# Low parts of MLP weights: negated high part plus an adding transfer, in place of a subtraction on GpSimd

## Chip, cores and metric

The kernel runs on one core of a Trainium2 chip. The metric is the device time of one execution in microseconds (us). The time before is the median of three runs, 1112.05 us.

## What is computed

One layer of a hybrid encoder on 512 tokens of width 1024, in float32: a token mixer (a Mamba-2 branch, windowed attention, gates, an output product) and then a squared-ReLU MLP with a hidden width of 4096. The change touches only the MLP:

```
h = rmsnorm(x, pre_mlp_norm[l])
f = jnp.square(jax.nn.relu(h @ w_mlp_in[l])) @ w_mlp_out[l]
x = x + rmsnorm(f, post_mlp_norm[l])
```

w_mlp_in is 1024 x 4096 and w_mlp_out is 4096 x 1024.

## The kernel before

**Split products.** TensorE multiplies in fp32r, which keeps fewer bits than float32. So every factor is split into a high part (the value rounded to fp32r) and a low part (the value less its high part), and each product is three matmuls, `mm3` in lines 350 to 354: high by high, high by low, low by high, added up in PSUM. A weight chunk of 128 partitions by 1024 columns (512 KB) is loaded from HBM into a raw tile `wr` (`chunk_raw`, line 399, on SP's queue). ScalarE rounds it into `wh` (line 419), and GpSimd subtracts, `wl = wr - wh`, in pieces of 256 columns (line 423). `wr`, `wh` and `wl` have three buffers each (RAW and SPL of line 27); chunk n takes the buffer of chunk n - 3 once the last matmul that reads it is done.

**The MLP.** The hidden width is cut into 32 blocks of 128, one "up quantum" each (`up_quantum`, lines 1335 and 1336, which calls `cm`): one chunk of w_mlp_in in 8 slices of 128 x 128, 24 matmuls into one PSUM bank. The first three up quanta are made in two halves of the tokens (`up_halves`). Then `up_done` squares the result. Blocks 0 to 23 form three parts of eight. The second product of such a part is "folded": a two by two block scheme with seven products in place of eight (`folded_quanta`). A folded product has two chunks of its own, made of w_mlp_out rows by sums and differences (tiles `wd` and `wt`), with ScalarE's rounding in line 1413 and GpSimd's subtraction in line 1416, four pieces of 256 columns a chunk; it too has 24 matmuls. The last part (blocks 24 to 31) is the plain quarter: eight chunks of w_mlp_out through the same `chunk_split` (`down_quanta`, line 1453).

**The order of the work.** In `build` (lines 1561 to 1566) each of the seven folded products of a part is followed by one up quantum of the next part, and an eighth up quantum stands at the part's end. So the rings of three `wh` and three `wl` buffers go round once per pair: two chunks for the folded product, one for the up quantum. An up quantum's chunk takes the buffers of the up quantum before it, and one folded product runs on TensorE between the two.

**The planner.** All instructions are recorded first. `Planner` (lines 76 to 275) then simulates them with a cost per instruction (`duration`) and deadlines counted back from TensorE's order (`deadlines`), and sets the order on every engine by list scheduling (`plan`): TensorE takes the earliest recorded matmul that is ready, the others the most urgent ready one. The order is fixed when the kernel is built; on the chip each engine runs its queue in that order and waits on semaphores.

Of the kernel before, what the change touches and what calls it, by code (L numbers as in the profile page):

```python
# [10 lines left out]
F32 = mybir.dt.float32  # L11
F32R = mybir.dt.float32r
AF = mybir.ActivationFunctionType
ALU = mybir.AluOpType
# [61 lines left out]
class Planner:  # L76
# [93 lines left out]
    def duration(self, n):  # L170

        i, e = self.ins[n], self.eng[n]
        outs, ins = self.operands(i.outs), self.operands(i.ins)
        size = lambda ap: math.prod(d[1] for d in list(ap.ap)[1:])
        w = max([size(a) for a in outs + ins])
        psum = any(a.tensor.name.startswith(("ps_", "pp_")) for a in outs + ins)
        kind = type(i).__name__
        if e == "PE":
            w = size(outs[0])
            if ins[0].dtype == F32R:  # L180
                return 13.5 + w / 2.4, False
            c = (2.2 + w / 1.2) if i.is_transpose else (4.4 + w / 0.6)
            return (c / 2 if i.tile_size[1] == 64 and outs[0].ap[0][1] == 64 else c), False
        if e == "SP":
            return (600 if list(outs[0].ap)[0][1] == 64 else 375), False
        wide = sum(1 for a in ins if size(a) == w and w > 1)
        columns = sum(1 for a in ins if size(a) == 1 and w > 1)
        if e == "ACT":
            c = (170 if psum else 205) + 0.82 * w + (175 if len(outs) > 1 else 0)
            return c + (85 if columns else 0) * (w < 512 or columns > 1), False  # L190
        if e == "POOL":
            if "pow" in str(getattr(i, "op", "")):
                return (1020 if w > 1 else 545), True
            return (190 if w <= 4 else 180 + 2.15 * w), bool(ins)
        if wide >= 2:
            return 158 + 1.04 * w + (45 if columns else 0), not psum
        if kind == "InstTensorScalarPtr" and not psum:
            return 220 + 0.51 * w, True
        return 150 + 1.04 * w, False

    def deadlines(self):

        at, t = {}, 0.0
        for n, e in enumerate(self.eng):
            if e == "PE":
                at[n] = t
                t += self.cost[n][0]
        late = [0.0] * len(self.ins)
        for n in reversed(range(len(self.ins))):
            e, c = self.eng[n], self.cost[n][0]  # L210
            if e == "PE":
                late[n] = at[n]
                continue
            c += 4000 if e == "SP" else 0
            late[n] = min([late[s] - self.AFTER[self.eng[s]] for s in self.post[n]] + [t + 5000.0]) - c
        return late

    def plan(self, wait=0.3):
        late = self.deadlines()
        left = [len(p) + len(q) for p, q in zip(self.pre, self.turn)]  # L220
        ready = [0.0] * len(self.ins)
        avail = {e: [] for e in self.OVERLAP}
        key = [n if self.eng[n] == "PE" else late[n] for n in range(len(self.ins))]
        for n, k in enumerate(left):
            if not k:
                avail[self.eng[n]].append(n)
        free = dict.fromkeys(self.OVERLAP, 0.0)
        port = {"DVE": 0.0, "POOL": 0.0}
        queue = 0.0
        order = {e: [] for e in self.OVERLAP}  # L230
        for _ in self.ins:
            best = None
            for e, some in avail.items():
                if some:
                    t = max(free[e], min(ready[n] for n in some))
                    if best is None or t < best[0]:
                        best = t, e
            t, e = best
            some = avail[e]
            n = min((n for n in some if ready[n] <= t), key=lambda n: (key[n], n))  # L240
            if e != "PE":
                m = min(some, key=lambda n: (key[n], n))
                if ready[m] <= t + wait * self.cost[n][0]:
                    n = m
            some.remove(n)
            order[e].append(n)
            t = max(t, ready[n])
            c, locks = self.cost[n]
            end = t + c
            if e == "SP":  # L250
                aps = self.operands(self.ins[n].outs)
                size = 4 * math.prod(d[1] for d in aps[0].ap)
                queue = max(queue, t + 900) + size / 230
                free[e], end = end, queue + 2000
            elif e == "PE":
                free[e], end = end, end + 160
            else:
                if locks:
                    other = "POOL" if e == "DVE" else "DVE"
                    end += max(0.0, port[other] - t - 145)  # L260
                    port[e] = end
                free[e] = end - self.OVERLAP[e]
            for s in self.post[n]:
                same = self.eng[s] == e == "PE"
                ready[s] = max(ready[s], free[e] if same else end + self.AFTER[self.eng[s]])
                left[s] -= 1
                if not left[s]:
                    avail[self.eng[s]].append(s)
            for s in self.next[n]:
                ready[s] = max(ready[s], t)  # L270
                left[s] -= 1
                if not left[s]:
                    avail[self.eng[s]].append(s)
        self.length = max(free.values())
        return order
# [10 lines left out]
class Trunk:  # L286
# [104 lines left out]
    def chunk_raw(self, i):  # L391
        if len(self.chunks[i]) == 2:
            self.chunks[i][0]()
            return
        src, kk, n, _ = self.chunks[i]
        raw = self.wp.tile([128, 1024], F32, tag="wr", name=self.name("wr"), bufs=RAW)
        self.tags[raw.tensor.name] = "wr", RAW
        self.raw[i] = raw[:, :kk * n]
        self.nc.sync.dma_start(raw[:, :kk * n].rearrange("p (k n) -> p k n", k=kk), src)

    def chunk_split(self, i):
        if len(self.chunks[i]) == 2:
            self.parts[i] = self.chunks[i][1]()
            return
        _, kk, n, eng = self.chunks[i]
        raw = self.raw.pop(i)
        m = kk * n
        hi = self.wp.tile([128, 1024], F32R, tag="wh", name=self.name("wh"), bufs=SPL)
        self.tags[hi.tensor.name] = "wh", SPL
        if eng == "both":  # L410
            view = hi[:, :2 * m].rearrange("p (k u n) -> p k u n", k=kk, u=2)
            r3 = raw.rearrange("p (k n) -> p k n", k=kk)
            self.nc.scalar.copy(view[:, :, 0], r3)
            self.nc.gpsimd.tensor_tensor(view[:, :, 1], r3, view[:, :, 0].bitcast(F32), op=ALU.subtract)
            self.parts[i] = view.rearrange("p k u n -> p k (u n)")
            return
        lo = self.wp.tile([128, 1024], F32R, tag="wl", name=self.name("wl"), bufs=SPL)
        self.tags[lo.tensor.name] = "wl", SPL
        self.nc.scalar.copy(hi[:, :m], raw)  # L419
        engines = {"v": self.nc.vector, "p": self.nc.gpsimd}  # L420
        for e, c in zip(eng, range(0, m, m // len(eng))):
            c = slice(c, c + m // len(eng))
            engines[e].tensor_tensor(lo[:, c], raw[:, c], hi[:, c].bitcast(F32), op=ALU.subtract)  # L423
        v = lambda t: t[:, :m].rearrange("p (k n) -> p k n", k=kk)
        self.parts[i] = (v(hi), v(lo))
# [907 lines left out]
        return i if part >= FOLDED else 8 * part + n // 2 + 4 * (n % 2)  # L1333

    def up_quantum(self, i):
        return self.cm(self.d_w_mlp_in[0], self.block(i) * 128, lambda: self.h2, lambda ps: self.up_done(ps, i))

    def up_halves(self, n):

# [113 lines left out]
    def down_quanta(self, part, j):  # L1453
# [13 lines left out]
        def chunk(k):  # L1467
            r0 = (8 * part + k) * 128
            src = self.d_w_mlp_out[0, r0:r0 + 256, j * 512:(j + 1) * 512]
            return src.rearrange("(k p) n -> p k n", p=128), 2, 512, "v" if j == 1 and k == 6 else "p"  # L1470

        def step(ks):
            def run(parts):
# [123 lines left out]
```

## Time and profile before

| | |
|---|---|
| Median of three runs (lowest, highest) | 1112.05 us (1110.24, 1113.28) |
| The profiled execution's own time | 1110.86 us |
| Its span, first to last instruction | 1108.8 us |
| TensorE (PE) busy | 1091.0 us, 98% |
| VectorE (DVE), ScalarE (ACT), GpSimd (POOL) busy | 716.8, 622.7, 775.3 us |
| Read from HBM | 124.59 MB |
| Mean granted clock of TensorE | 0.995 |

PE is TensorE's matmuls, PEld its weight loads, SP the queue that issues the transfers. A row of a group gives the count behind an x, then the busy time, the mean of one, and the idle time of the engine just before with what ended it. A row of the timeline gives start, length, engine, line, operation, and the tiles written and read. Matmuls overlap, so the step from one start to the next (0.227 us at 512 columns) says how fast they go, not their length of 0.39 us.

### The profile page before, as it was taken

The numbers are of one execution on the slowest core, as the hardware profiler recorded it, in microseconds if no ns is written. First come the engines' busy times: TensorE is split into PE (matmuls) and PEld (weight loads), VectorE is DVE, ScalarE is ACT, GpSimd is POOL, SyncE is SP. The second block draws the span as 40 slices with busy tenths as digits, with TensorE's granted clock in tenths as the row PEclk, the third lists the DMA queues.
The fourth block names the chain that finished last, engine by engine and source line by source line (L and its number), as shares of the span: only waits on it lengthen the run. The fifth ranks groups of instructions, "written<-read, shape, count | busy, mean of one in ns | idle before, by whom it ended". The sixth has DMA issues, their size and how long they took to land.

```text
span 1108.8 us, 16609 instructions
## 1 busy us (share of the span) xinstructions
PE 1091.0 (98%) x5651; PEld 912.0 (82%) x5651; DVE 716.8 (65%) x1245; ACT 622.7 (56%) x1325; POOL 775.3 (70%) x946
## 2 busy tenths in 40 slices
PE   8999999999999999999999899999999999999997
PEld 6988888888888888888888688889888888888886
DVE  6297788787796778787875863334555665564235
ACT  5456676786677667667678533323554444444331
POOL 4536557567667888998979976521679898898842
PEclk8999999999999999999999999999999999999999
DMA  6434443534534536354555463513312522523232
GB/s 185 140 92 128 120 110 82 145 95 113 117 109 122 135 87 176 112 134 132 148 141 148 123 186 111 175 52 97 107 46 77 171 57 77 171 57 95 65 107 76
DMA packets 207583, 128.08 MB, mean 116 GB/s; under 512 B 10851, under 2 KB 192595, under 8 KB 207500
## 3 DMA queue, kind: packets, MB, share of 16 engines
q1 hardware_dynamic: 207500, 127.04, 41.1%
q8 instruction: 44, 0.72, 0.3%
q14 instruction: 39, 0.32, 0.1%
HBM read 124.59 MB, written 2.42 MB: 115 GB/s over the span
## 4 chain that ended last, share of the span: by engine, by line
PE 95%; DVE 1%; POOL 1%; ACT 1%; DMA 1%; issue 1%; SPq 0%; POOLq 0%; DVEq 0%
PE pp L344 69%; PE ps L344 22%; PE ps L348 3%; DMA ident<-in_cst 1%; POOL wl L423 0%; POOL w L1066 0%; DVE x L1512 0%; POOL frs L1508 0%; PE pp L348 0%; SPq L516 0%; POOL ssq L1075 0%; ACT junk L1498 0%; DVE acc L1496 0%; DVE wd L1384 0%; ACT n L1036 0%
## 5 line engine op out<-in xcount | busy, mean ns | idle before, releaser
L423 POOL TENSOR_TENSOR wl<-wr,wh 128x256 fp32r<-128x256 f32 (+1 forms) x513 | 443.0, 890 | 176.8 <-ACT wh L419 174.2
L344 PE MATMUL pp<-h,wh 128*128 128x512 f32 (+1 forms) x1760 | 538.3, 389 | 2.3 <-DVE ft L1320 1.8
L344 PEld LDWEIGHTS pp<-h,wh 128*128 128x128 f32 x1760 | 321.1, 188 | 68.3 <-issue 4.1
L344 PE MATMUL pp<-h,wl 128*128 128x512 f32 (+1 forms) x872 | 335.7, 385 | 0.2 <-POOL wl L423 0.2
L419 ACT CAST wh<-wr 128x1024 fp32r<-128x1024 f32 (+1 forms) x141 | 146.7, 1042 | 178.7 <-PE pp L344 122.5
L344 PEld LDWEIGHTS pp<-h,wl 128*128 128x128 f32 x872 | 163.7, 188 | 34.8 <-POOL wl L423 0.9
L1416 POOL TENSOR_TENSOR wl<-wd,wh 128x256 fp32r<-128x256 f32 x144 | 117.5, 852 | 13.4 <-ACT wh L1413 11.9
L344 PE MATMUL ps<-wl,fh 128*128 128x512 f32 (+1 forms) x192 | 73.0, 380 | 0.0
L344 PE MATMUL ps<-wh,fh 128*128 128x512 f32 (+1 forms) x192 | 73.0, 380 | 0.0
L344 PE MATMUL ps<-wh,fl 128*128 128x512 f32 (+1 forms) x192 | 73.0, 380 | 0.0
L1413 ACT CAST wh<-wd 128x512 fp32r<-128x512 f32 x72 | 41.5, 618 | 31.3 <-PE ps L344 19.8
L1065 POOL TENSOR_TENSOR w<-w,E 128x256 f32<-128x256 f32 x48 | 39.9, 834 | 23.9 <-DVE w L1063 22.9
L1036 ACT ACTIVATE n<-cb,tables 128x128 f32<-128x128 f32 x128 | 49.3, 392 | 7.7 <-DVE cb L1027 4.3
L344 PE MATMUL pp<-yh,wl 128*128 128x512 f32 x128 | 49.8, 390 | 1.6 <-POOL wl L423 1.6
L868 DVE SCALAR_TENSOR_TENSOR u<-pp,cv,u 128x510 f32<-128x510 f32 (+1 forms) x64 | 47.7, 746 | 4.0 <-ACT u L864 2.8
L1037 ACT ACTIVATE m<-cb,tables 128x128 f32<-128x128 f32 x128 | 49.1, 390 | 1.2 <-DVE u L875 0.8
L344 PE MATMUL pp<-yl,wh 128*128 128x512 f32 x128 | 49.7, 389 | 0.0
L344 PE MATMUL pp<-yh,wh 128*128 128x512 f32 x128 | 49.6, 389 | 0.0
L1032 ACT ACTIVATE rf<-rf,tables 128x128 f32<-128x128 f32 x128 | 42.2, 393 | 11.4 <-DMA rf<-csT 9.7
L966 POOL TENSOR_TENSOR xd<-x,tables 128x256 f32<-128x256 f32 x48 | 33.1, 707 | 15.5 <-ACT x L891 13.4
L800 ACT ACTIVATE P<-P,mx 128x384 f32<-128x384 f32 (+1 forms) x64 | 35.2, 551 | 12.9 <-DVE mx L797 12.7
L1284 DVE SCALAR_TENSOR_TENSOR pp<-pp,r 128x256 f32<-128x256 f32 (+1 forms) x24 | 13.5, 563 | 44.6 <-ACT r L1280 44.3
(244 smaller groups left out, 2071.4 us busy)
## 6 DMA issues: line engine op xcount, KB each, us to landing
wr<-in_w_in SPq DMA_DIRECT2D x76, 512.0 KB, 4.0
wr<-in_w_mlp_in SPq DMA_DIRECT2D x32, 512.0 KB, 4.0
wd<-in_w_mlp_out SPq DMA_DIRECT2D x48, 256.0 KB, 3.0
rf<-csT SPq DMA_DIRECT2D x32, 256.0 KB, 4.0
rb<-csT SPq DMA_DIRECT2D x32, 256.0 KB, 3.3
wr<-in_w_ssd_out SPq DMA_DIRECT2D x14, 512.0 KB, 4.4
E<-csE SPq DMA_DIRECT2D x96, 64.0 KB, 3.9
x<-in_x SPq DMA_DIRECT2D x16, 256.0 KB, 5.7
```

The costliest lines, as they stand in the source:

```text
L344: self.nc.tensor.matmul(out, lhsT, rhs, start=start, stop=stop, skip_group_check=more)
L348: self.nc.tensor.transpose(out, src, self.ident[:n, :n])
L419: self.nc.scalar.copy(hi[:, :m], raw)
L423: engines[e].tensor_tensor(lo[:, c], raw[:, c], hi[:, c].bitcast(F32), op=ALU.subtract)
L800: nc.scalar.activation(p[:, :w], p[:, :w], AF.Exp, bias=mx[:, n:n + 1], accum_out=sm[:, n:n + 1])
L868: nc.vector.scalar_tensor_tensor(u[:, a:e], ps[:, a + d:e + d], self.wtap(t, b), u[:, a:e], op0=ALU.mult, op1=ALU.add)
L1032: nc.scalar.activation(v4(rf)[:, h], v4(rf)[:, h], AF.Identity, bias=ncs[:, 0, h:h + 1])
L1036: nc.scalar.activation(v4(n)[:, h], cb[:, 0], AF.Copy, scale=dt[:, 0, h:h + 1])
L1037: nc.scalar.activation(v4(m)[:, h], cb[:, 1], AF.Copy, scale=dt[:, 1, h:h + 1])
L1065: nc.gpsimd.tensor_tensor(w, w, E[:, d], op=ALU.add)
L1413: nc.scalar.copy(hi[:, cols], src)
L1416: (nc.vector if q == 512 else nc.gpsimd).tensor_tensor(lo[:, c], src[:, e * q:(e + 1) * q], hi[:, c].bitcast(F32), op=ALU.subtract)
```

## The change

Up quanta 3 to 31 (29 chunks) and seven of the eight chunks of the plain quarter make `wl` in another way. ScalarE writes the negated high part into `wl` (a second pass over 128 x 1024, new line 424). Then GpSimd's queue issues a transfer that reads the same weights from HBM once more and adds them onto `wl` in SBUF (new line 425), which gives `wr - wh` as before. GpSimd's subtraction of these 36 chunks goes. The first three up chunks, the folded products and one chunk of the plain quarter stay. The planner counts such a transfer as 1000 ns on GpSimd and 3000 ns until it has landed.

```diff
+        if e == "POOL" and "DMA" in kind:
+            return 1000, False
...
-            c += 4000 if e == "SP" else 0
+            c += 4000 if e == "SP" else 3000 if "DMA" in type(self.ins[n]).__name__ else 0
...
+                end += 3000 if "DMA" in type(self.ins[n]).__name__ else 0
...
-        self.raw[i] = raw[:, :kk * n]
+        self.raw[i] = raw[:, :kk * n], src
...
-        raw = self.raw.pop(i)
+        raw, src = self.raw.pop(i)
...
         self.nc.scalar.copy(hi[:, :m], raw)
+        if eng == "dma":
+            self.nc.scalar.activation(lo[:, :m], hi[:, :m].bitcast(F32), AF.Copy, scale=-1.0)
+            self.nc.gpsimd.dma_start(lo[:, :m].rearrange("p (k n) -> p k n", k=kk), src, accum_op=ALU.add)
+            eng = ""
         engines = {"v": self.nc.vector, "p": self.nc.gpsimd}
-        for e, c in zip(eng, range(0, m, m // len(eng))):
+        for e, c in zip(eng, range(0, m, m // max(1, len(eng)))):
...
-        return self.cm(self.d_w_mlp_in[0], self.block(i) * 128, lambda: self.h2, lambda ps: self.up_done(ps, i))
+        return self.cm(self.d_w_mlp_in[0], self.block(i) * 128, lambda: self.h2, lambda ps: self.up_done(ps, i), "dma")
...
-            return src.rearrange("(k p) n -> p k n", p=128), 2, 512, "v" if j == 1 and k == 6 else "p"
+            return src.rearrange("(k p) n -> p k n", p=128), 2, 512, "v" if j == 1 and k == 6 else "dma"
```

With these, lines from 344 on carry numbers 3 to 7 higher (line 344 becomes 347, 419 becomes 422, 1413 becomes 1420), and buffer numbers shift.

GpSimd's queue in the middle of the first folded part, before: the last pieces of one folded product, the four pieces of an up chunk, the eight of the next folded product (x2 stands for two equal rows).

```order
L1416 TENSOR_TENSOR wl_9163<-wd_8856,wh_9162 128x256 x2
L1416 TENSOR_TENSOR wl_9163<-wd_8858,wh_9162 128x256 x2
L423 TENSOR_TENSOR wl_9226<-wr_9152,wh_9225 128x256 x4
L1416 TENSOR_TENSOR wl_9265<-wd_9221,wh_9264 128x256 x2
L1416 TENSOR_TENSOR wl_9265<-wd_9223,wh_9264 128x256 x2
L1416 TENSOR_TENSOR wl_9273<-wd_9258,wh_9272 128x256 x2
L1416 TENSOR_TENSOR wl_9273<-wd_9260,wh_9272 128x256 x2
```

The same place after:

```order
L1423 TENSOR_TENSOR wl_9145<-wd_8844,wh_9144 128x256 x2
L1423 TENSOR_TENSOR wl_9145<-wd_8846,wh_9144 128x256 x2
L425 DMA wl_9208<-in_w_mlp_in 128x8x128
L1423 TENSOR_TENSOR wl_9245<-wd_9203,wh_9244 128x256 x2
L1423 TENSOR_TENSOR wl_9245<-wd_9205,wh_9244 128x256 x2
L1423 TENSOR_TENSOR wl_9253<-wd_9238,wh_9252 128x256 x2
L1423 TENSOR_TENSOR wl_9253<-wd_9240,wh_9252 128x256 x2
```

One transfer stands where four subtractions stood, between the same neighbours.

ScalarE's queue at the same place, before: the roundings of a folded product (from `wd`), then of the up chunk (from `wr`), then the up quantum's ReLU (`r`).

```order
L1413 CAST wh_9162<-wd_8856 128x512
L1413 CAST wh_9162<-wd_8858 128x512
L419 CAST wh_9225<-wr_9152 128x1024
L1280 ACTIVATE r_9195<-pp_9170 128x512
L361 CAST fh_9200<-pp_9170 128x256
```

After:

```order
L1420 CAST wh_9144<-wd_8844 128x512
L1420 CAST wh_9144<-wd_8846 128x512
L422 CAST wh_9207<-wr_9134 128x1024
L424 ACTIVATE wl_9208<-wh_9207 128x1024
L1287 ACTIVATE r_9177<-pp_9152 128x512
```

The negation stands right behind the rounding, ahead of the ReLU.

TensorE's queue at the start of the same up quantum, before (`pp` is the up quantum's bank, `ps` the banks of folded products):

```order
L344 MATMUL ps_9125<-wh_9162,fl_8795 128x512
L344 MATMUL pp_9280<-h_887_8192,wh_9225 128x512
L344 MATMUL pp_9280<-h_888_8193,wh_9225 128x512
L344 MATMUL pp_9280<-h_887_8192,wl_9226 128x512
L344 MATMUL pp_9280<-h_889_8194,wh_9225 128x512
```

After:

```order
L347 MATMUL ps_9107<-wh_9144,fl_8785 128x512
L347 MATMUL pp_9260<-h_887_8192,wh_9207 128x512
L347 MATMUL pp_9260<-h_888_8193,wh_9207 128x512
L347 MATMUL ps_9294<-wh_9244,fh_8489 128x512
L347 MATMUL ps_9295<-wh_9244,fh_8489 128x512
L347 MATMUL ps_9294<-wl_9245,fh_8489 128x512
L347 MATMUL ps_9294<-wh_9244,fl_8490 128x512
L347 MATMUL pp_9260<-h_887_8192,wl_9208 128x512
L347 MATMUL pp_9260<-h_889_8194,wh_9207 128x512
```

Ahead of the up quantum's first matmul that reads `wl`, four matmuls of the next folded product were drawn forward. Over the seven up quanta that follow the folded products of this part their number is 1, 1, 2, 3, 4, 4 and 0, and 0 for the eighth.

## Prediction

> **What bounds the kernel now.** First the page's busy times, then the windows over the MLP (length, then busy time of PE, PEld, DVE, ACT and POOL, then granted clock, share of the DMA engines, GB/s).
>
> ```profile
> PE 1091.0 (98%) x5651; PEld 912.0 (82%) x5651; DVE 716.8 (65%) x1245; ACT 622.7 (56%) x1325; POOL 775.3 (70%) x946
> 770.00:790.00 20.00, 18.25 (x136) 17.29 (x135) 13.05 (x28) 10.45 (x20) 10.64 (x15) 1.00 0.35 102
> 813.00:1057.00 244.00, 244.00 (x1078) 201.93 (x1077) 128.50 (x199) 111.64 (x189) 213.35 (x258) 1.00 0.31 96
> 1047.00:1080.00 33.00, 33.00 (x147) 27.31 (x146) 9.48 (x13) 11.01 (x17) 16.95 (x10) 1.00 0.35 112
> 1080.00:1109.00 29.00, 21.70 (x119) 18.74 (x117) 16.33 (x30) 5.60 (x14) 5.87 (x5) 0.93 0.19 73
> ```
>
> From 813 to 1057 us, the folded parts, PE is busy 244.00 of 244.00 us at full clock. POOL is busy 213.35 there, 87%, and nobody on the path waits for it. The chain that ended last says the same: quantum after quantum of PE, each 5.44 us, up quanta in `pp`, folded products in `ps`.
>
> ```profile
> 883.73 10.88 PE pp L344 x48
> 894.61 5.44 PE ps L344 x24
> 900.05 5.44 PE pp L344 x24
> ```
>
> So a lighter POOL has nothing to give in this stage. What counts is how close a weight chunk comes to being late. The timeline of one round (one up quantum's end to the next one's start) shows it, on PE, ACT and POOL:
>
> ```profile
> 894.22 0.39 PE L344 MATMUL pp<-h,wl 128*128 128x512 f32 x1
> 894.45 0.39 PE L344 MATMUL ps<-wh,fh 128*128 128x512 f32 x1
> 899.89 0.62 PE L344 MATMUL pp<-h,wh 128*128 128x512 f32 x2
> 900.34 0.39 PE L344 MATMUL pp<-h,wl 128*128 128x512 f32 x1
> ...
> 894.55 1.05 ACT L419 CAST wh<-wr 128x1024 fp32r<-128x1024 f32 x1 [2.31 <-PE pp L344]
> 895.51 0.59 ACT L1280 ACTIVATE r<-pp 128x512 f32<-128x512 f32 x1
> ...
> 895.68 3.05 POOL L423 TENSOR_TENSOR wl<-wr,wh 128x256 fp32r<-128x256 f32 x4 [0.37 <-ACT wh L419]
> 899.50 6.53 POOL L1416 TENSOR_TENSOR wl<-wd,wh 128x256 fp32r<-128x256 f32 x8 [0.77 <-ACT wh L1413]
> ```
>
> The last matmul of an up quantum starts at 894.22. It frees the buffers, and ACT rounds the next up chunk from 894.55 (it waited for PE). POOL has all four pieces of `wl` by 898.73. PE runs one folded product and reads the new `wl` at 900.34. The last piece is 1.6 us early, and the first, which alone is needed at 900.34, much more.
>
> **The change, part by part.** *Removed:* POOL's pieces.
>
> ```profile
> L423 POOL TENSOR_TENSOR wl<-wr,wh 128x256 fp32r<-128x256 f32 x98 | 83.6, 883 | 19.6 <-ACT wh L419 19.5
> PE pp L344 <- DVE ft L1320: 1.8, 1, 1.8
> ```
>
> Some 84 us of POOL go in this stage, 0 from the path, since PE waits for none of it. The one PE wait in the MLP that a lighter POOL might touch, through a quicker DVE, is the 1.8 us at its start (second row, from the waits after 785); PE idles 1.75 us from 770 to 790. So the gain is between 0 and 1.8 us, and I take 0, as DVE's own chain makes that wait.
>
> *Added on ACT:* a pass over 128 x 1024. No row shows the negation; the rounding of the same size takes 1.05, the next instruction starting 0.96 us after it. It begins at 895.51 and ends at 896.56. ACT is busy 111.64 of 244 us, so it has room for 25 more (24 up chunks). But on the round it costs its full 1.0 us, between buffer free and `wl` ready.
>
> *Added on POOL's queue and DMA:* the adding transfer can start at 896.56, since it needs the negated part in place, and must have landed whole by 900.34, since every slice hangs on one semaphore. That leaves 3.8 us. While POOL waits for ACT here, only the folded product's pieces stand behind it, and in the trace those begin at 899.50, later than the wait ends: no cost. For the landing, the nearest rows are SP's plain transfers in the same stage (count, size, median us from issue to landing; below them least, median and most for `wr`):
>
> ```profile
> wr<-in_w_mlp_in SPq DMA_DIRECT2D x21, 512.0 KB, 4.0
> wd<-in_w_mlp_out SPq DMA_DIRECT2D x36, 256.0 KB, 2.9
> wr<-in_w_mlp_out SPq DMA_DIRECT2D x5, 512.0 KB, 3.6
> DMA to landing us min/median/max: 3.6/4.0/4.2
> ```
>
> The same bytes in the same shape, without the addition, take 4.0 us: already 0.2 more than there is. From 256 to 512 KB in long rows costs 0.7, so 1.4 us of 512 KB is data, and 0.4 more in these short rows (512 bytes, 1024 of them): data 1.8, fixed 2.2. An adding transfer reads its destination too. Bounds: data once (4.0 in all; down to 3.6 by the fastest row), read twice (2.2 + 3.6 = 5.8), three passes (2.2 + 5.4 = 7.6). What POOL needs to issue it no row shows: from no more than SP, whose issue lies inside the 4.0, up to 1024 rows at POOL's pace per element, 0.742 us for 256:
>
> ```profile
> L423 POOL TENSOR_TENSOR wl<-wr,wh x98: 728/742/2393, 814.1 to 1053.4; 128x256 fp32r<-128x256 f32 x96, 128x1024 fp32r<-128x1024 f32 x2
> 898.76 0.38 SPq L399 DMA_DIRECT2D wr<-in_w_mlp_in  x1
> ```
>
> That is 0 to 3.0 us; I take 0, by SP's own issue, the nearest instruction. `wr` is now freed by ACT at 895.6 and no longer by POOL (second row: SP reloaded it at 898.76, when POOL was done), so the next load runs beside the adding transfer: 0 to 1.8 us more; I take 0, as it starts a microsecond ahead. Ends 3.6 and 7.6 + 3.0 + 1.8 = 12.4; value 5.8.
>
> The Trainium skill, *DMA: Bandwidth & Descriptors*, section "Anatomy of one DMA — SWDGE (gpsimd) path", gives transfers from GpSimd's queue about 2.0 us plus bytes over 436 GB/s: 3.2 us here, an estimate; by it nothing waits and the sum below is 0. No run here has such a transfer, and the plain one's 4.0 us speaks for more.
>
> *Moved on PE:* the matmuls drawn forward fill the gap, but only once. What is drawn ahead of one up quantum is missing between it and the next, so a round keeps its length: latency plus the 22 matmuls left. The order shows this, needing 1, 1, 2, 3, 4, 4 and then 0. Each part pays the fill back at its end; I take 0 for it.
>
> **The sum.** A round lasts 10.88 us while the landing X is under 3.8, else X - 3.8 more. Three parts of seven rounds: 21 x (5.8 - 3.8) = 42.0. The eighth up quantum's chunk starts its round during the seventh, so its wait is hidden but for one small rounding of ACT's (about 0.4) set ahead of its negation: 3 x 0.4 = 1.2. Up quantum 3 follows two half quanta in place of a folded product, the same 5.4 us; it would wait 2.0, of which 1.8 is the wait for DVE already there: 0.2. Quanta 4 to 7 have one quantum more between: 0. In the plain quarter five of the seven chunks have two quanta (10.9 us) and the sixth too; the seventh, in the last triple, has 5.44 + 1.36 + 0.23 = 7.0 less 2.0 on ACT, so 5.0 for 5.8: 0.8. Together 44.2. Against the profiled execution's 1110.86 us (span 1108.8, 2.1 around it) that is 1155; the median of the runs is 1.2 above the profiled one, so 1156.
>
> **The rivals.** *It fits.* X stays at or under 3.9: POOL's transfer lands as the fastest plain one (3.6), and the addition is free. For it: the DMA engines are only 31% busy in this stage, so a second read may cost little. Against: the median plain landing is 4.0. Then 21 x 0.1 = 2 us at most, and DVE's 1.8 may come back: 1110 to 1115, about 1112. This is the case that does not end slower; it decides at X = 3.8. The rule of the Trainium skill's DMA page above would make this case certain; it has the chance given below.
>
> *POOL makes the transfer slowly.* At the 3.0 us of its pace per element X is 8.8 and a round loses 5.0: 105 us, with the smaller terms (1.2, 3.2 and 3.8) about 1225. It decides from an issue of some 2 us on. For it: 1024 rows is a lot for a program; against: SP's issue takes 0.38. Then PE's gaps last 5 us. With idle time in it, the last window's granted clock is 0.93, against 1.00 in the full ones; 0.93 on the 5 us after each gap adds 21 x 0.35 = 7. The Trainium skill, *TensorE: Matmul & The Clock Gate*, Part 1, has the clock halved after about 3.4 us of idleness; my own gaps of 2.0 us stay under that, these don't.
>
> *The order gains.* POOL's and DVE's shared waits go and nothing is late: at most the 1.8 us above, within the noise. No separate time.
>
> **How the numbers follow.** About 0.3%, 3.3 us, is what a measurement of this kernel can tell. Waiting rounds with X from 4.0 to 8.0 (1118 to 1207, with the smaller terms): 0.66; it fits: 0.15, of which 0.03 is faster than 1108.7 and 0.12 the same; a slow POOL, over 1207: 0.19. So faster 0.03, same 0.12, slower 0.85. The time is the likeliest case's, 1156. The range goes from 1113, about the middle of the fitting case, to 1240, X = 9.4 (21 x 5.6 = 118 and 10 in the smaller terms): about 0.08 lies below and 0.08 above. The likeliest case alone is 1118 to 1207.
>
> **What would show it.** In the changed profile: the negation at about 1.05 us, 36 of them; POOL's 36 transfers, their landing 5.8 us by median; PE idle at the first `wl` matmul of an up quantum, released by DMA, 2.0 us in 21 places, and rounds of 12.9 in place of 10.88; PE's busy share from 813 on down to 85%; POOL near 660 us busy (36 chunks less: 29 x 3.5 and 7 x 2.4), ACT near 660 (36 x 1.05 more); HBM read 143.5 MB (36 x 0.524 more). A landing under 3.8, or PE still unbroken, would make it wrong; so would gaps of 4 us and more, or a wait on POOL's pieces for the folded products in place of the transfer.

## The result and the profile after

| | before | after |
|---|---|---|
| Median of the compared runs (lowest, highest) | 1111.14 us (1109.97, 1113.28) | 1241.15 us (1240.65, 1253.78) |
| Profiled execution, its span | 1110.86, 1108.8 us | 1240.69, 1238.8 us |
| Mean granted clock | 0.995 | 0.959 |

The changed kernel takes 1.1192 times as long, with a 95% interval of 1.1146 to 1.1237: 130 us more, where the forecast was 44 us more and the range ended at 1240. The page of the changed kernel, busy times and HBM:

```profile
PE 1137.0 (92%) x5651; PEld 935.1 (75%) x5651; DVE 712.0 (57%) x1245; ACT 658.1 (53%) x1361; POOL 713.1 (58%) x859
HBM read 143.46 MB, written 2.42 MB: 118 GB/s over the span
```

PE has the same 5651 matmuls and is busy 46 us longer, in a span 130 us longer: 84 us are new idle time, 46 us are slower matmuls. The windows of the changed kernel show where. The stage that took 244.00 us before, from the first folded product to the last up quantum, now runs from 821 to 1186 us. Ahead of it stands the first part's up stage, behind it the plain quarter.

```profile
770.00:821.00 51.00, 45.36 (x251) 39.54 (x251) 27.79 (x59) 27.02 (x50) 16.04 (x16) 0.93 0.71 134
821.00:1186.00 365.00, 286.48 (x1079) 223.37 (x1078) 126.68 (x199) 137.64 (x215) 165.30 (x186) 0.89 0.51 101
1186.00:1232.00 46.00, 44.78 (x220) 37.57 (x218) 17.21 (x33) 18.06 (x29) 8.77 (x8) 1.00 0.59 125
```

The folded stage is 121 us longer: 78.5 us in which PE is idle, and 42.5 us because 1079 matmuls take 286.48 us and not 244.00, at a granted clock of 0.89. The start of the MLP (43 us before, 770 to 813) takes another 8 us. The plain quarter is as long as before to about 1 us.

The waits after 770 us (total, times, longest) name one main releaser for PE (DVE, POOL and a chunk of w_mlp_out add 1.7, 1.4 and 1.2 us), and the new instructions by tile give their lengths (least, median, most in ns; the last row in us):

```profile
PE pp L347 <- DMA wl<-in_w_mlp_in: 80.4, 23, 7.8
```

```profile
L424 ACT ACTIVATE wl<-wh x36: 1056/1061/1069, 781.4 to 1209.6; 128x1024 fp32r<-128x1024 f32 x36
L425 POOL DMA_DIRECT2D wl<-in_w_mlp_in x29: 1540/1564/1756, 782.8 to 1171.6; - x29
L425 POOL DMA_DIRECT2D wl<-in_w_mlp_out x7: 1188/1192/1197, 1173.6 to 1210.9; - x7
DMA to landing us min/median/max: 5.7/6.7/11.8
```

So the adding transfer keeps POOL for 1.56 us to issue it (1.19 for a chunk of w_mlp_out, which has 256 rows and not 1024) and lands 6.7 us after the issue begins. One round in the timeline, as a chain:

```profile
944.26 1.05 ACT L422 CAST wh<-wr 128x1024 fp32r<-128x1024 f32 x1 [3.03 <-PE pp L347]
945.34 0.37 SPq L402 DMA_DIRECT2D wr<-in_w_mlp_in  x1
945.34 1.06 ACT L424 ACTIVATE wl<-wh 128x1024 fp32r<-128x1024 f32 x1
946.76 1.56 POOL L425 DMA_DIRECT2D wl<-in_w_mlp_in  x1 [4.01 <-ACT wl L424]
949.68 0.61 PE L347 MATMUL pp<-h,wh 128*128 128x512 f32 x2
953.28 0.65 PE L347 MATMUL pp<-h,wl 128*128 128x512 f32 x1 [2.76 <-DMA wl<-in_w_mlp_in]
953.73 1.05 PE L347 MATMUL pp<-h,wh 128*128 128x512 f32 x2
954.59 0.63 PE L347 MATMUL pp<-h,wl 128*128 128x512 f32 x1
955.01 1.05 PE L347 MATMUL pp<-h,wh 128*128 128x512 f32 x2
...
957.03 0.39 PE L347 MATMUL pp<-h,wl 128*128 128x512 f32 x1
957.26 0.63 PE L347 MATMUL pp<-h,wh 128*128 128x512 f32 x2
957.73 0.39 PE L347 MATMUL pp<-h,wl 128*128 128x512 f32 x1
```

Two things stand here. PE waits 2.76 us for the landing. And behind the wait three matmuls take 1.28 us (953.73 to 955.01, 0.43 each) where they took 0.70 from 957.03 to 957.73: until about 957 the matmuls go at half speed. The 22 matmuls behind this wait take 6.74 us, and 5.1 at full speed. In the folded stage there are 21 such waits (the first at 830.03, the last at 1174.29), together 80.3 us from start to start less one matmul's 0.227; behind 17 of them the next 22 matmuls are slow, 33 us in all.

The trace's own record of the granted clock says when. The clock changes only at steps of 3.413 us, counted through the whole execution; every stretch at half clock, up to the last matmul, lasts one, two or three such steps. Here are five of these windows in the changed kernel, in the columns of the windows above: two at the wait that ended at 953.28, and three at a wait of 2.38 us that ended at 917.62.

```profile
950.06:953.47 3.41, 0.65 (x4) 0.23 (x3) 2.88 (x6) 2.00 (x4) 3.41 (x5) 1.00 1.00 123
953.47:956.88 3.41, 3.41 (x9) 2.63 (x9) 0.81 (x1) 0.16 (x1) 2.28 (x3) 0.50 0.00 0
912.51:915.92 3.41, 2.22 (x9) 1.21 (x7) 1.67 (x4) 1.81 (x4) 3.39 (x5) 1.00 1.05 144
915.92:919.33 3.41, 1.71 (x7) 1.43 (x8) 0.00 (x0) 0.00 (x0) 2.65 (x4) 1.00 0.70 178
919.33:922.75 3.42, 3.42 (x16) 2.81 (x15) 0.69 (x1) 0.00 (x0) 0.00 (x0) 1.00 0.27 93
```

Ahead of the slow window PE was busy for 0.65 of 3.41 us. The wait at 917.62 falls across a border: PE was busy for 2.22 and 1.71 us of the two windows that share it, and the clock stayed full. Counted over the fifteen traces of this case, from 800 us on, a window that follows one at full clock is at half clock in 135 of 135 cases where PE was busy for under 43% of the window before, in 13 of 48 cases from 43 to 52%, and in none of 1271 above. So a wait costs slow matmuls when it leaves PE busy for less than about half of one such window. Whether a wait of 2 to 4 us does that depends on where it falls.

Fifteen of the 21 waits last 2.6 to 3.4 us. Four last 5.9 to 7.9. One of these four rounds in the timeline and in the DMA view of 994 to 1006 us (median us to landing last):

```profile
995.61 1.57 POOL L425 DMA_DIRECT2D wl<-in_w_mlp_in  x1 [8.62 <-ACT wl L424]
996.67 2.44 SPq L1384 DMA_DIRECT2D wd<-in_w_mlp_out  x4
1005.43 0.79 PE L347 MATMUL pp<-h,wl 128*128 128x512 f32 x1 [5.69 <-DMA wl<-in_w_mlp_in]
```

```profile
wd<-in_w_mlp_out SPq DMA_DIRECT2D x4, 256.0 KB, 7.7
wl<-in_w_mlp_in POOLq DMA_DIRECT2D x1, 512.0 KB, 9.8
```

Here SP sends off four loads for folded chunks 1 us behind POOL's issue, and the transfer lands after 9.8 us. In the other three long rounds such loads begin 0.6 to 1.3 us behind the issue: four of them in one (landing 10.1 us), eight in the other two (11.2 and 11.8). In the remaining 17 rounds SP sends off nothing in the first 1.9 us behind the issue.

### The profile page after: what moved, and what is told of

It is laid out like the page before. It is cut to its first block, busy times and chain, and to the rows that moved or that the text cites. A ratio compares the mean times of both kernels' runs of the same rounds, so it can differ in the third digit from the quotient of the medians.

```text
span 1238.8 us, 16580 instructions
## 1 busy us (share of the span) xinstructions
PE 1137.0 (92%) x5651; PEld 935.1 (75%) x5651; DVE 712.0 (57%) x1245; ACT 658.1 (53%) x1361; POOL 713.1 (58%) x859
## 3 DMA queue, kind: packets, MB, share of 16 engines
HBM read 143.46 MB, written 2.42 MB: 118 GB/s over the span
## 4 chain that ended last, share of the span: by engine, by line
PE 64%; issue 12%; DMA 11%; POOL 5%; DVE 4%; ACT 3%; SPq 0%; POOLq 0%; DVEq 0%; ACTq 0%
PE pp L347 51%; PE ps L347 11%; DMA wl<-in_w_mlp_in 10%; POOL wl L1423 3%; PE ps L351 2%; ACT wh L422 1%; DVE u L875 1%; DMA wl<-in_w_mlp_out 0%; ACT wl L424 0%; DVE Q L775 0%; DMA x<-in_x 0%; POOL wl L430 0%; POOL w L1073 0%; DVE x L1519 0%; DVE P L798 0%
## 5 line engine op out<-in xcount | busy, mean ns | idle before, releaser
L347 PE MATMUL pp<-h,wh 128*128 128x512 f32 (+1 forms) x1760 | 562.7, 404 | 2.1 <-DVE ft L1327 1.7
L347 PE MATMUL pp<-h,wl 128*128 128x512 f32 (+1 forms) x872 | 353.1, 405 | 80.6 <-DMA wl<-in_w_mlp_in 80.4
L430 POOL TENSOR_TENSOR wl<-wr,wh 128x256 fp32r<-128x256 f32 (+1 forms) x390 | 332.3, 878 | 128.4 <-ACT wh L422 126.0
L347 PEld LDWEIGHTS pp<-h,wh 128*128 128x128 f32 x1760 | 337.8, 198 | 74.3 <-issue 4.1
L347 PEld LDWEIGHTS pp<-h,wl 128*128 128x128 f32 x872 | 172.3, 198 | 126.7 <-DMA wl<-in_w_mlp_in 79.8
L425 POOL DMA_DIRECT2D wl<-in_w_mlp_in x29 | 45.5, 1569 | 196.7 <-ACT wl L424 156.9
L1458 DVE TENSOR_TENSOR acc<-acc,ps 128x512 f32<-128x512 f32 x40 | 27.0, 682 | 121.6 <-PE ps L347 121.4
```

The costliest lines, as they stand in the source:

```text
L347: self.nc.tensor.matmul(out, lhsT, rhs, start=start, stop=stop, skip_group_check=more)
L425: self.nc.gpsimd.dma_start(lo[:, :m].rearrange("p (k n) -> p k n", k=kk), src, accum_op=ALU.add)
L1458: self.nc.vector.tensor_tensor(self.acc[t, j], self.acc[t, j], ps, op=op)
```

## The experiments

The theory after the result: PE waits for the landing of the adding transfer, which is 6.7 us because of its issue, the addition, and loads beside it; and a wait above some length also makes the matmuls behind it slow. The rivals: the negation on ACT costs it, the moved order of PE costs it, or the loss of clock has another cause than the waits. "After" is the changed kernel throughout; ratios are against the kernel before, with 95% intervals.

**The negation alone.** It stays, and POOL adds the raw tile to it in SBUF, with no transfer.

```diff
-            self.nc.gpsimd.dma_start(lo[...], src, accum_op=ALU.add)
+            for q in range(0, m, 256):
+                c = slice(q, q + 256)
+                self.nc.gpsimd.tensor_tensor(lo[:, c], raw[:, c], lo[:, c].bitcast(F32), op=ALU.add)
```

> The negation on ScalarE stays, the adding transfer goes: GpSimd adds the raw tile onto the negated part, four pieces of 256 columns. Theory (the transfer's landing is the cost): 1110 to 1116 us, as the last piece was 1.6 us early and the pass takes 1.0. Rival (the added pass on ScalarE between buffer free and low part is what makes the round late): 1125 us or more.

1112.75 us, ratio 1.0012 (1.0002 to 1.0023). The window of the folded stage:

```profile
813.00:1057.00 244.00, 244.00 (x1078) 202.03 (x1077) 134.40 (x202) 137.11 (x213) 212.67 (x263) 1.00 0.33 93
```

PE is unbroken again, with ACT at 137.11 us. The extra pass is paid only where something behind it is late.

**Only where a second quantum covers it.** Up quanta 3 to 7 and the plain quarter keep the adding transfer; the others go back to POOL's subtraction.

```diff
-        ... self.up_done(ps, i), "dma")
+        ... self.up_done(ps, i), "dma" if i < 8 else "pppp")
```

> Adding transfers only where a chunk has two quanta or nearly two of cover: up quanta 3 to 7 and the seven chunks of the plain quarter (12 of 36); up quanta 8 to 31 are subtracted on GpSimd as before. Theory (only short cover costs): one wait at up quantum 3 (some 4 us and 2 us of half speed behind it) and about 1 us in the last triple, 1114 to 1122 us. Rival (each such transfer costs wherever it stands): a third of the 130 us, 1154 us.

1118.45 us, 1.0063 (1.0046 to 1.0080). The folded stage's rounds hold the cost; the start and the plain quarter are worth 7 us.

**Slots for every second chunk.** From up quantum 9 on, the chunk of every odd one goes to four slot tiles of its own, outside the rings of three, by two half transfers. So it can be made before the up quantum ahead of it is done.

```diff
+    def half_split(self, raw, src, q):
+        hi, lo = self.slots.get("vh", dtype=F32R), self.slots.get("vl", dtype=F32R)
+        self.nc.scalar.copy(hi, raw[:, q * 128:(q + 4) * 128])
+        self.nc.scalar.activation(lo, hi.bitcast(F32), AF.Copy, scale=-1.0)
+        self.nc.gpsimd.dma_start(lo.rearrange("p (k n) -> p k n", k=4), src[:, q:q + 4], accum_op=ALU.add)
...
+                       "slots" if i > 8 and i % 2 else "dma")
```

> Every second up chunk from block 9 on has its high and low part in tiles of its own (four of 512 columns, so two transfers of half the size), so the shared rings go round once in two rounds and an up chunk has two quanta (10.9 us) of cover in place of one. Same negations, same bytes added. Theory (the cover is what fails): 1112 to 1125 us, TensorE unbroken in most rounds. Rival (the transfers, their issue on GpSimd or the second pass on ScalarE cost time wherever they stand): near 1241 us.

1147.04 us, 1.0308 (1.0284 to 1.0333): three quarters of the loss is gone, but it missed its range. The waits of PE in this run:

```profile
PE pp L347 <- DMA wl<-in_w_mlp_in: 22.0, 7, 4.9
```

Seven waits are left of 23, one of them at the start of the MLP. Longer cover removes most. In four of the six that are left in the folded stage the transfer landed only after 10.4 to 13.2 us, with other transfers and loads beside it. The slots also bring half transfers, which by themselves shorten waits (the run in two halves below), so this run alone doesn't give the worth of the cover.

**A plain transfer.** No addition; the low part then holds the whole weight, which leaves the subtraction out.

```diff
-  ... self.nc.gpsimd.dma_start(lo[...], src, accum_op=ALU.add)
+  ... self.nc.gpsimd.dma_start(lo[...], src)
```

> The same transfer from GpSimd's queue without the addition: it overwrites the negated part, so the low part holds the whole weight and the result is not the reference's. Theory (the addition makes the data part read twice, 1.8 us): landing 4.9 us in place of 6.7, some 1.8 us less wait in each of 23 places and fewer slow steps, 1165 to 1190 us. Rival (the addition is free, and it is the issue on GpSimd and the busy DMA engines that make the transfer long): landing 6.5 us, 1230 to 1241 us.

1178.76 us, 1.0598 (1.0563 to 1.0634). The low-part tiles and the waits of PE:

```profile
L425 POOL DMA_DIRECT2D wl<-in_w_mlp_in x29: 873/913/1097, 780.2 to 1110.1; - x29
L425 POOL DMA_DIRECT2D wl<-in_w_mlp_out x7: 696/700/707, 1112.1 to 1148.2; - x7
DMA to landing us min/median/max: 4.1/5.2/10.3
```

```profile
PE pp L347 <- DMA wl<-in_w_mlp_in: 42.4, 22, 6.2
```

POOL's queue alone makes a 512 KB transfer land after 5.2 us, against 4.0 on SP's. The addition adds 1.5: 0.65 in the issue (1.564 less 0.913), the other 0.85 behind it. Half the waiting goes, and with waits of mostly 1.1 to 1.9 us most slow matmuls go too.

**Short waits made shorter.** Eight unused matmuls (1.8 us) open 21 of the up quanta, where PE would wait.

```diff
-    def cm(self, w, c, act, done, eng="pppp"):
+    def cm(self, w, c, act, done, eng="pppp", warm=0):
+            for _ in range(warm):
+                self.mm(ps, parts[0][0][:, 0], a[0][0], True, True)
...
+        ... self.up_done(ps, i), "dma", 8 * (i > 7 and i % 8 < 7))
```

> Eight unused matmuls of 512 columns (1.8 us) open each of the 21 up quanta that follow a folded product, in the bank that the real ones then overwrite. Theory (a round waits for its weights, and after a gap of over 2 us TensorE runs some 3 us at half speed): the waits keep their sum with the filling counted, the half speed goes; about 1200 us, 40 less than the changed kernel's 1241, with TensorE's granted clock in the stage at 0.97 or more. Rival (TensorE is slower for another reason, such as the added transfers' traffic): nothing is won, 1241 us or up to 38 us more, and the steps behind the waits stay at 0.43 us.

1212.51 us, 1.0902 (1.0872 to 1.0932): more matmuls, and 29 us less than after, where 40 less were expected. A round in its timeline, and the window of 100 us around it:

```profile
1060.62 0.47 PE L347 MATMUL pp<-h,wl 128*128 128x512 f32 x1 [1.50 <-DMA wl<-in_w_mlp_in]
1060.93 0.62 PE L347 MATMUL pp<-h,wh 128*128 128x512 f32 x2
1061.39 0.39 PE L347 MATMUL pp<-h,wl 128*128 128x512 f32 x1
1061.62 0.61 PE L347 MATMUL pp<-h,wh 128*128 128x512 f32 x2
```

```profile
1050.00:1150.00 100.00, 89.54 (x389) 72.03 (x388) 29.73 (x44) 41.52 (x59) 49.78 (x57) 1.00 0.51 99
```

Three matmuls take 0.69 us (1060.93 to 1061.62) straight behind the wait, and the granted clock is 1.00. So the slow matmuls belong to the long waits. They are no price of the landing itself, which is 6.7 us here as well.

**Half as many of them.** Four unused matmuls in place of eight.

> Four unused matmuls (0.9 us) in place of eight (1.8 us) open the same 21 up quanta, so the idle stretch that is left is about 2.0 to 2.4 us in place of 1.3 to 1.9. Theory (matmuls run at half speed for some us only after an idle stretch longer than a bound that lies between 1.9 and 2.6 us): the end of the round is set by the landing, so nothing is paid for the four fewer; with the gaps below the bound 1209 to 1217 us, as with eight, with the gaps above it at half speed 1222 to 1236. Rival (the loss grows with the length of the stretch from zero): some slow matmuls after nearly every gap, 1218 to 1230 us, with 22 matmuls taking 5.6 to 6.2 us.

1228.38 us, 1.1057 (1.1037 to 1.1078). The waits came out at 2.4 to 2.9 us, not 2.0 to 2.4, and after 9 of the 17 that are not among the long ones the next 22 matmuls take 6.7 us, after the other 8 they take 5.1. No value between, so the rival (a loss growing from zero) falls; so does a sharp bound on the length of a wait between 1.9 and 2.6 us. At equal length it is sometimes paid and sometimes not, by where the wait falls on the windows of 3.413 us (above). The wait at 917.62 in the changed kernel itself is one that is not:

```profile
917.62 0.51 PE L347 MATMUL pp<-h,wl 128*128 128x512 f32 x1 [2.38 <-DMA wl<-in_w_mlp_in]
917.97 0.63 PE L347 MATMUL pp<-h,wh 128*128 128x512 f32 x2
918.44 0.39 PE L347 MATMUL pp<-h,wl 128*128 128x512 f32 x1
```

**No matmuls drawn forward.** The planner counts a landing as 1.5 us later and not 3, which puts PE's order back to that of the kernel before.

```diff
-                end += 3000 if "DMA" in type(self.ins[n]).__name__ else 0
+                end += 1500 if "DMA" in type(self.ins[n]).__name__ else 0
```

> The planner counts 1500 ns in place of 3000 until such a transfer has landed, and draws no matmul of a folded product forward: TensorE's order is that of the kernel before. Theory (drawn matmuls fill a gap only once, a round keeps its length): 1236 to 1247 us, with longer single waits of about 3.5 us. Rival (each drawn matmul hides 0.23 us for good): 45 of them over three parts, some 10 us more, 1251 us.

1233.7 us, 1.1101 (1.1079 to 1.1123): a little below its range. The moved matmuls gained nothing. The waits of PE for the up weights are as long in all as in the changed kernel:

```profile
PE pp L347 <- DMA wl<-in_w_mlp_in: 81.6, 22, 6.1
```

What is less is matmul time: PE is busy 1126.8 us here and 1137.0 in the changed kernel, with 17 windows at half clock from 800 us on and not 24.

**Smaller loads beside it.** The loads for the folded chunks bring 64 of 512 columns, and VectorE zeroes the rest, which leaves out 7/8 of those weights.

```diff
-            nc.sync.dma_start(raw[name, k], self.d_w_mlp_out[0, r0:r0 + 128, j * 512:(j + 1) * 512])
+            nc.sync.dma_start(raw[name, k][:, :64], self.d_w_mlp_out[0, r0:r0 + 128, j * 512:j * 512 + 64])
+            nc.vector.memset(raw[name, k][:, 64:], 0.0)
```

> The folded products' loads bring 64 of 512 columns, the rest is set to zero on VectorE, so the result is not the reference's; all else as in the changed kernel. Theory (the landings of 10 to 12 us are those that meet four loads of 256 KB each): no landing over 8 us, the four waits of 6 to 8 us become 3, 1220 to 1230 us. Rival (long landings come from the transfers themselves): 1238 us or more.

1229.18 us, 1.1061 (1.1021 to 1.1100).

```profile
PE pp L347 <- DMA wl<-in_w_mlp_in: 68.9, 22, 5.2
```

The waits of 5.9 to 7.9 us are gone, the longest is 5.4 from start to start, and their sum falls by 11.5. The median time falls by 12, the profiled executions' by 8 (1240.69 to 1232.51); PE is busy 1140.1 us in that one, 3 us more than in the changed kernel's.

**The negated part first.** ACT negates straight from the raw tile, ahead of the rounding, so that POOL can issue a microsecond earlier.

```diff
+        if eng == "dma":
+            self.nc.scalar.activation(lo[:, :m], raw, AF.Copy, scale=-1.0)
         self.nc.scalar.copy(hi[:, :m], raw)
         if eng == "dma":
-            self.nc.scalar.activation(lo[:, :m], hi[:, :m].bitcast(F32), AF.Copy, scale=-1.0)
```

> ScalarE makes the negated part straight from the raw weights and ahead of the high part, so the transfer can start one pass (1.0 us) sooner; the same work otherwise. Theory (the round is the chain from buffer free to landing, and TensorE runs slow only behind gaps of more than about 2 us): 22 us of waits go, and most gaps fall from 3 to 2 us, so part of the 46 us of slow matmuls goes too: 1185 to 1205 us. Rival (no clock threshold, only the chain): 1219 us. Rival (the chain is not the bound): 1241 us.

1249.04 us, 1.1239 (1.1202 to 1.1276): no faster than after (the two intervals overlap), where a gain was expected; the theory as it stood fell here. A round in its timeline, and the issues in its DMA view of 850 to 1150 us:

```profile
965.68 1.06 ACT L423 ACTIVATE wl<-wr 128x1024 fp32r<-128x1024 f32 x1 [7.00 <-PE pp L347]
966.64 1.03 ACT L424 CAST wh<-wr 128x1024 fp32r<-128x1024 f32 x1
967.10 1.56 POOL L426 DMA_DIRECT2D wl<-in_w_mlp_in  x1 [6.31 <-ACT wl L423]
967.70 0.37 SPq L402 DMA_DIRECT2D wr<-in_w_mlp_in  x1
```

```profile
wl<-in_w_mlp_in POOLq DMA_DIRECT2D x19, 512.0 KB, 8.0
```

The issue did come earlier: 1.42 us behind the start of ACT's first pass, not 2.50 (944.26 to 946.76). But the raw tile is now given back later than the issue, so SP's next load starts 0.6 us behind POOL's issue, where in the changed kernel it started 1.42 us ahead (945.34). The landing takes 8.0 us. That suggested a collision, which three runs were to settle.

**The negation from the raw tile, meant to come second.**

```diff
-            self.nc.scalar.activation(lo[:, :m], hi[:, :m].bitcast(F32), AF.Copy, scale=-1.0)
+            self.nc.scalar.activation(lo[:, :m], raw, AF.Copy, scale=-1.0)
```

> The order on ACT is that of the changed kernel (high part first, negation second); the one edit is that the negation reads the raw tile, with the same rounding, in place of the high part. So nothing on the round's chain is longer, but the raw tile is given back after the second pass, 1.06 us later, and SyncE's load of the next raw tile then starts beside GpSimd's adding transfer. Theory (the load of the next raw tile beside the adding transfer is what took the gain in the run with the negated part first, where the transfer landed after 8.0 us in place of 6.6): the landing is about 8 us here too, the waits at the first low-part matmul of a round go from about 2.9 us to 3.8 to 4.5 us, and the time is 1260 to 1285 us. Rival (in that run it was the later high part or the moved order, not the load): landing 6.5 to 6.9 us as in the changed kernel, time 1236 to 1248 us.

1241.82 us, 1.1176 (1.1149 to 1.1204). The run did not separate anything: with no tie between the two passes the planner put the negation first (in ACT's timeline at 962.07 us, the rounding at 963.03), so it is the run before once more (landing 8.1 us, waits of 86.3 us in all, 85.6 there). Its PE is busy 1138.5 us, and 1145.9 there: two kernels with the same waits differ by 7 us in how slow the matmuls behind them are (29 windows at half clock from 800 us on, and 33 there).

**The suspected load made small, in both orders.** SP brings an eighth of each raw tile of the up weights and VectorE zeroes the rest.

```diff
+        if self.chunks[i][3] == "dma" and kk == 8:
+            self.nc.sync.dma_start(raw[:, :n], src[:, 0])
+            self.nc.vector.memset(raw[:, n:kk * n], 0.0)
+            return
```

> The kernel with the negated part made first, straight from the raw tile, with one edit: SyncE loads an eighth of each raw tile of the up weights (one block of 128 rows) and VectorE zeroes the rest, which leaves out 7/8 of the high parts of the up weights (the adding transfer still moves whole chunks). The order on PE, ACT and POOL is the same. Theory (the load of the next raw tile, which there starts 0.6 us after GpSimd's issue in place of 1.4 us before it, lengthens the landing from 6.7 to 8.0 us): the landing is 5.9 to 6.8 us, the wait at the first low-part matmul falls from 3.7 to about 1.8 to 2.4 us, and with fewer slow matmuls the time is 1175 to 1210 us. Rival (something else in that order lengthens the landing): it stays at 7.7 us or more, 1235 to 1250 us.

> The changed kernel with the same edit: an eighth of each raw tile of the up weights is loaded, the rest zeroed on VectorE, which leaves out 7/8 of the high parts of the up weights. Theory (the load is over, or nearly, when the adding transfer's data start, since it is issued 1.4 us ahead of GpSimd's issue): the landing falls little, from 6.7 to 6.0 to 6.6 us, and the time to 1215 to 1240 us, so that the two orders change places: the negated part first is the faster one by 20 us or more. Rival (the load has no part in it): 1234 to 1246 us here, and the order with the negated part first stays the slower one.

With the negated part first 1186.24 us, 1.0665 (1.0640 to 1.0690); in the changed kernel's order 1244.88 us, 1.1183 (1.1149 to 1.1218), above its range of 1215 to 1240. With whole loads the two orders differed by no more than the noise (1249.04 and 1241.82 us against 1241.15); with small ones the negated part first is faster by 59 us. The issues and the waits with the negated part first:

```profile
wl<-in_w_mlp_in POOLq DMA_DIRECT2D x21, 512.0 KB, 6.7
```

```profile
PE pp L347 <- DMA wl<-in_w_mlp_in: 52.6, 21, 4.0
```

The landing is back at 6.7 us, so the 1.3 us were the load beside it. In the changed kernel's order the load costs nothing: 6.8 us without it. Most waits of the faster run are 2.2 to 2.9 us, and slow matmuls follow 8 of 21, against 21 of 21 with the load.

**Two halves.** The adding transfer is made as two of half the rows.

```diff
+            v = lo[:, :m].rearrange("p (k n) -> p k n", k=kk)
+            for q in range(0, kk, kk // 2):
+                self.nc.gpsimd.dma_start(v[:, q:q + kk // 2], src[:, q:q + kk // 2], accum_op=ALU.add)
```

> Each adding transfer is made as two, of half the rows, each with its own completion. Theory (the wait is the landing of the low part, a sum of issue, fixed time and data that is read twice): the first half is issued in about 1.3 us and lands after about 4.6 us (6.7 less 0.3 of issue and 1.8 of data), so the wait falls from 2.9 to about 0.9 us; its 12 matmuls take 2.6 us, by which the second half (issued 1.3 us later, landing about 6 to 7 us after the first issue) is there. 21 times 0.9 is 19 us, no slow matmuls after such gaps: 1130 to 1165 us with the rounds in which other loads collide. Rival (two transfers cost the fixed part twice, one after the other): the second lands at 9 us or later, a second wait of about 2 us in each round, 1180 to 1215 us.

1172.46 us, 1.0548 (1.0507 to 1.0589), between the two ranges. The low-part tiles and the waits:

```profile
L427 POOL DMA_DIRECT2D wl<-in_w_mlp_in x58: 1276/1711/2402, 781.3 to 1101.8; - x58
```

```profile
PE pp L347 <- DMA wl<-in_w_mlp_in: 25.6, 21, 2.6
```

The waits for the up weights fall from 80.4 to 25.6 us without any earlier start: PE waited for the whole chunk where it needed a slice. But half a chunk keeps POOL for 1.71 us by median, more than a whole one (1.564); the two are 3.4 us on POOL, and PE now waits more for POOL's folded pieces (6.4 us, 1.4 in the changed kernel).

## Why the prediction was wrong in size

*Right.* The mechanism of the wait, the sign and the places. A lighter POOL gave nothing. The folded stage has 21 waits, all for the landing of `wl`; the eighth up quantum of a part hardly waits (0.2 us in one part, nothing in the other two); the plain quarter costs 1 us (0.8 was said). The negation is 36 times 1.06 us, ACT 658.1 us (660), HBM 143.46 MB (143.5).

*Wrong: the landing X.* The step was "value 5.8", with "fixed 2.2", data read twice, "I take 0" for POOL's issue and "I take 0" for the load beside it. X is 6.7 by median. The issue of 1.56 us lay between the ends named, 0 and 3.0, and SP's instruction was the wrong nearest row for it: a 512 KB transfer costs POOL 0.91 us even without the addition (the plain transfer run). The packets of one round say the same. SP's plain load of 945.34 has its first packet 1.03 us and its last one's end 3.51 us behind the issue; the adding transfer of 946.76 has them at 2.27 and 6.18. So the start is 1.2 us later, which was put at 0, and the data take 1.4 us longer, where 1.8 was said. With X = 6.7 the waits should be 2.9 us; the median of the 21 is 3.1. The 3.8 us of slack also left out the hand-over from ACT to POOL, 0.36 us in the round shown (negation ends at 946.40, issue starts at 946.76). Together that is 20 us more than the forecast 42.

*Wrong: the loads beside it.* The load of `wr` was rightly put at 0, since it starts ahead (the pair with small `wr` loads). The loads that do collide are SP's groups of four `wd`, which the prediction did not look at. Six waits of 4.3 to 7.9 us come to 18 us above six of 3.0, and 15 of that lie in the four longest, where such groups are sent off. The other two, 4.35 and 4.29 us, have ordinary landings of 6.7 and 6.6 us. They are the seventh rounds of the first two parts and belong to the fill (below). Making the `wd` loads small took 11.5 us of waits away. Three waits of 4.3 to 5.4 us stayed there: two are again the seventh rounds, one of them with a landing of 7.5 us, and what lengthens the third (a landing of 7.7 us with no load of SP's issued near it) is open.

*Wrong: the clock.* The step was "my own gaps of 2.0 us stay under that, these don't". Had the gaps been 2.0 it would nearly have held. But the bound it used, 3.4 us of idleness, is not where the loss begins. In the eleven kernels here that have such waits (the one in halves left out), from 800 us on, the 22 matmuls behind a wait for `wl` of an up quantum are slow after 2 of 40 waits under 2.3 us, after 93 of 131 from 2.3 to 4.0, and after all 49 above. The size was off too: the rival put 0.35 us on a gap, from a window's mean clock; here it is 33 us on 21 waits, 1.6 each.

The windows in the section on the result give the reason: what counts is how much of a window of 3.413 us PE is busy, with the bound between 43 and 52%. A wait that ends inside one window needs 1.6 to 1.9 us of idleness for that (48 to 57% of it); one that is cut by a border needs up to twice as much.

The Trainium skill, *TensorE: Matmul & The Clock Gate*, Part 1, gives an activity window of 3413 ns that runs freely, and the halved clock after an idle window. The traces agree on the window. They differ on the idleness: a window in which PE is busy for up to 43% is enough.

*The sum, mended.* Folded stage: 42 + 20 + 18 is 80 us of waits from start to start (78.5 us as idle time), and 42.5 us of slower matmuls, of which 33 stand directly behind the waits. With 8 us at the start and the rest within 1 us that is the 130. At the start only 0.2 was said, as DVE's wait of 1.8 us was to lie within the new one. It does not:

```profile
PE pp L347 <- DVE ft L1327: 1.7, 1, 1.7
```

PE still waits 1.7 us for DVE and then, two matmuls on, another 4.1 us for the landing, and the 22 matmuls behind that take 7.3 us, 2.2 too many. That is 6.3 of the 8; the rest was not looked into. The landing of this chunk takes 9.0 us, with two more adding transfers issued 4.0 and 6.0 us behind it.

*POOL's time.* It was put near 660 us and is 713.1: 29 issues of 1.57 us and 7 of 1.19 are 54 us, the same 0 that was wrong in X.

*The fill* (the matmuls drawn forward). It was taken at 0, and the waits bear that out. Before the first six waits of the first part 1, 1, 2, 3, 4 and 4 matmuls are drawn forward and before the seventh none; that one lasts 4.35 us at a landing of 6.7, and so it goes in the second part (4.29 us). There the fill is paid back, and without it the waits add up to the same (81.6 and 80.4 us). Without it the kernel is 7 us faster. That is no more than two kernels with equal waits differed by, through slow matmuls (the negated part first, and the run that repeated it), so these runs don't say whether the moved order costs anything.

*A rule that had to be measured.* The Trainium skill, *DMA: Bandwidth & Descriptors*, section "Anatomy of one DMA — SWDGE (gpsimd) path", puts such a transfer at 3.2 us, an estimate from its figures; the runs show 5.2 plain and 6.7 adding, in rows of 512 bytes. By the page nothing would have waited.

## What to carry over

Count the slack from "source ready" to "first use" in one round before work is moved to a transfer: 3.8 us were enough for a subtraction in four pieces, each usable when done, and not for one transfer that is usable only whole. A transfer issued by GpSimd costs that engine time, in part by its rows, and again for an addition, and what other queues send off in the following microsecond belongs in its landing time. Where a round is to get a new wait, price it twice: as idle time, and as slow matmuls behind it wherever it leaves PE busy for less than about half of a window of 3.413 us. Here that befell 2 of 40 waits under 2.3 us and all 49 above 4.0.

## What the hardware showed that was not expected

- POOL is kept 0.91 us by a plain transfer of 1024 rows of 512 bytes and 0.70 us by one of 256 rows of 2 KB; 1.56 and 1.19 us with an addition. Two transfers of half the rows, back to back, take 1.71 us each by median.
- A landing is 6.7 us by median, 8.0 with one 512 KB load issued 0.6 us later, and 9.8 with four 256 KB loads issued 1 us later, though the DMA engines' mean share of busy time in the stage is 0.51. That mean hides full stretches: in the window of 950.06 to 953.47, while a transfer lands, it is 1.00.
- TensorE's granted clock changes only at steps of 3.413 us. Behind a window at full clock in which PE was busy for under 43% the next one was at half clock every time, behind one over 52% never. Two kernels with equal waits differed by 7 us through slow matmuls; from 800 us on, one has 33 windows at half clock and the other 29.
